# Hybrid encoder layer: another form of the bidirectional scan's inner products, and its state products in each other's banks

## Chip, cores and metric

One Trainium2 chip, one core. The metric is device time in microseconds (us) for one execution of the program.

## What is computed

One encoder layer on x of 1024 tokens × 1024 features, fp32. After an RMSNorm one projection gives all mixers their columns. Mixer A is a convolution branch. Mixer B, which this change is about, is a gated linear recurrence in both directions, with 8 heads of 128 features. Then both are gated, merged and projected, and a feed-forward layer with a short convolution and a last RMSNorm follow. The recurrence, per head and direction:

```python
f = lb + (1.0 - lb) * sigmoid(z);  f = clip(f, 1e-6, 1.0)      # one forget value per token and feature
k = (1.0 - lb) * sigmoid(-z);      q = silu(q) * 128 ** -0.5
S_t = diag(f_t) S_{t-1} + k_t v_t^T                            # 128 x 128 state
o_t = S_t^T q_t                                                # forward + backward (tokens flipped)
o = o * rsqrt(mean(o * o) + 1e-6) * norm_w * silu(og)          # per head, then @ o_w
```

So token t sees token s through q_t · (the product of all f between them) · k_s, per feature.

## The kernel before, in words

**Dense work.** Projections are matmuls of 128x128 weights by 128x512 tokens. Each fp32 operand is split into a high and a low part and multiplied in three terms (`mm3`, L148 to L150). The matmul of 128x512 is about 0.39 us in the trace. Much of the dense work (merge gates and the convolution branch's projection) is kept as a stream, `dense`, which hands out *pieces*; a piece is two steps of k, six matmuls. `dense.fill(n)` runs n pieces, with fractions carried over.

**The scan.** 8 heads × 2 halves of 512 tokens make 16 *units*. Features lie in partitions, tokens along the free axis, both directions side by side (128 x 2 x 512). A unit has these parts:

- `scan_inputs` loads q and z (SP's queue), makes f (sigmoid, then Identity with scale and bias on ScalarE, ACT; clip on VectorE, DVE, L1103) and k (sigmoid of −z, L1093 to L1096).
- `scan_base` (DVE) works in blocks of 8 tokens: running products of f inside a block (`DE`), their reciprocal (L1127), q and k scaled by them (`Qh`, and `Kh` at L1074), then q and k decayed to the block's edges (`qF`, `kG`) and the blocks' totals `tb`. It is a generator of 12 steps. All products go through the helper at L1071.
- `scan_levels` puts together the 32x32 and larger blocks of the token × token matrix. `inside` (L1203) multiplies `Qh` and `Kh` per 32 tokens for both directions. Then come levels h = 8, 16, 32, 64: at each, the second half of a block of 2h tokens sees the first half, and the reverse. Levels 8 and 16 need k in an order of its own, which ACT copies into a page `A` (L1189, two pages) and 16 small matmuls read (L1191); levels 32 and 64 multiply directly (`blocks`, L1217), after a matmul by zeros (`none`, L1241) has cleared the bank. After each level, `kG`, `qF` and `tb` are doubled to the next block size (L1071). Masks choose which product goes where in `D_t` (L1255 to L1261), and ACT puts `D_t` on the diagonal of the matrix `S_t` (L1263, four copies at L1265).
- `scan_states` transposes `kG` (L1275, ACT copies the result at L1277) and multiplies by v (L1284). The forward product goes into bank `ob`, from which DVE makes the states `Sf` (L1290, L1292). The backward product goes into `sc`, from which ACT copies `Sb` (L1302, L1304).
- `scan_outputs`, once per head, multiplies S_t by v and q by the states (L1325), ACT copies and squares the result (L1327, L1330), GpSimd (POOL) makes the root of the mean (`rstd_small`, L519 and L520), ACT scales (L1344), PE transposes (L1351), DVE gates (L1353).

**Order.** TensorE's (PE) instructions run in the order in which the program writes them. The other engines' orders are chosen by a scheduler that estimates times; it keeps the data's order. Every generator's `yield` is a *filler place*: the loop calls `between(FILL)` there, which lets in dense pieces, steps of the next unit's base (`BASE_STEPS`) and one step of the last head's outputs:

```python
def between(fill):
    dense.fill(fill)
    if ahead is not None:
        ahead.step(BASE_STEPS)
    pending.fill(1)
```

`scan_levels` has four places and `scan_states` three, with FILL = 1.265 pieces each; ahead of the first unit stands `dense.fill(21)`. Outputs of a head run in the places of the next head's first unit and into its second.

**PSUM.** 8 banks of 128x512: three for dense products (`mm`), two `sc`, two `tr` (transposes), one `ob`. A bank is written again only when its readers are done; with one bank of a kind, the next writer waits for the last reader.

Of the kernel before, what the change touches and what calls it, by code (L numbers as in the profile page):

```python
# [10 lines left out]
F32 = mybir.dt.float32  # L11
F32R = mybir.dt.float32r
I32 = mybir.dt.int32
U8 = mybir.dt.uint8
# [5 lines left out]
FILL = 1.265  # L20
# [10 lines left out]
BASE_STEPS = 2  # L31
# [16 lines left out]
def tile_hybrid_encoder(  # L48
# [877 lines left out]
    m_f, m_b, m_d, m_16 = [cp.tile([P, 32], U8, name=n) for n in ("m_f", "m_b", "m_d", "m_16")]  # L926

    def build_masks():
# [7 lines left out]
        fs = mp.tile([P, 4, 32], F32, tag="tm", name=nm("fs"), bufs=4)  # L936
        V.tensor_copy(fs[:, 0, :], xo)
        V.tensor_tensor(fs[:, 1, :], it, ip, op=ALU.subtract)
        ge = fs[:, 1, :]
        V.tensor_scalar(m_d, fs[:, 0, :], 0.0, None, op0=ALU.is_equal)  # L940
        V.tensor_scalar(m_16, fs[:, 0, :], 16.0, None, op0=ALU.is_ge)
        V.tensor_scalar(fs[:, 2, :], fs[:, 0, :], 8.0, None, op0=ALU.is_lt)
        V.tensor_scalar(fs[:, 3, :], ge, 0.0, None, op0=ALU.is_ge)
        V.tensor_tensor(m_f, fs[:, 2, :], fs[:, 3, :], op=ALU.mult)
        V.tensor_scalar(fs[:, 3, :], ge, 0.0, None, op0=ALU.is_lt)
        V.tensor_tensor(m_b, fs[:, 2, :], fs[:, 3, :], op=ALU.mult)
# [111 lines left out]
    NB = H // 8  # L1058
    DE = hp.tile([P, 2, 2, H], F32, name="DE")
    dg = hp.tile([P, 4, 32], F32, name="dg")  # L1060
    none = hp.tile([P, 32], mybir.dt.bfloat16, name="none")
    E0, D0 = 0, 2 * H
    for o in (E0 + 3, D0 + 3):
        G.memset(view(DE, o, [[8, 2 * NB]]), 1.0)
    G.memset(none, 0.0)
    G.memset(dg, 0.0)

    N2 = 2 * NB

    def tt(o, a, b, op=ALU.mult):  # L1070
        V.tensor_tensor(o, a, b, op=op)  # L1071

    def keys(o, a, scale, b):
        V.scalar_tensor_tensor(o, a, scale, b, op0=ALU.mult, op1=ALU.mult)  # L1074
# [7 lines left out]
    def scan_inputs(i):  # L1082


        h, half = divmod(i, 2)
        q = page(hp, "q", 2)
        f = hp.tile([P, 2, H], F32, tag="f", name=nm("f"), bufs=2)
        kk = hp.tile([P, 2, H], F32, tag="k", name=nm("k"), bufs=2)
        nc.sync.dma_start(q, d_q[h][half])
        for d in range(2):  # L1090
            z = page(hp, "zi", 3)
            nc.sync.dma_start(z, d_z[d][h][half])
            A.activation(kk[:, d, :], z, AF.Sigmoid, scale=-1.0)  # L1093
            A.activation(z, z, AF.Sigmoid)
            fo = view(f, d * H + 7 * d, [[8, NB], [1 - 2 * d, 8]])
            A.activation(  # L1096
                fo,
                z.rearrange("p (b e) -> p b e", e=8),
                AF.Identity,
                scale=oml_of(d, h),  # L1100
                bias=lb_of(d, h),
            )
        V.tensor_scalar(f, f, MIN_FORGET, 1.0, op0=ALU.max, op1=ALU.min)  # L1103
        return q, f, kk, kscale[:, h : h + NH + 1 : NH]

    def scan_base(ins):


        q, f, kk, ks = ins

        def two(t, *r):
            if len(r) == 1:
                return view(t, r[0], [[8, N2]])
            return view(t, r[0], [[r[1] - r[0], 2], [8, N2]])

        fv = lambda *r: two(f, *r)
        ed = lambda *r: two(DE, *r)
        D = D0


        V.tensor_copy(ed(2, D + 4), fv(3, 4))
        tt(ed(1, D + 5), fv(2, 4), fv(3, 5))
        yield
        tt(ed(0, D + 6), fv(1, 6), ed(1, D + 5))
        tt(ed(D + 7), ed(D + 6), fv(7))
        yield
        V.reciprocal(ed(D, 7), ed(0, D + 7))  # L1127
        yield

        fm = hp.tile([P, 2, NB], F32, tag="fm", name=nm("fm"), bufs=2)  # L1130
        turned = view(fm, NB, [[-NB, 2], [1, NB]])
        tt(turned, view(f, 0, [[H, 2], [8, NB]]), view(DE, E0, [[H, 2], [8, NB]]))
        tb = hp.tile([P, 3, NB], F32, tag="tb", name=nm("tb"), bufs=3)
        tt(tb[:, 0:2, :], turned, view(DE, D + 7, [[H, 2], [8, NB]]))
        V.tensor_copy(tb[:, 2, :], tb[:, 0, :])
        tt(ed(D + 1, 6), ed(D, 7), fv(1, 7))
        yield
        tt(ed(D + 2, 5), ed(D + 1, 6), fv(2, 6))
        tt(ed(4), ed(5), fv(5))
        yield  # L1140

        qF = hp.tile([P, 2, H], F32, tag="qF", name=nm("qF"), bufs=3)
        kG = hp.tile([P, 2, H], F32, tag="kG", name=nm("kG"), bufs=2)
        Qh = hp.tile([P, 2, H], F32, tag="Qh", name=nm("Qh"), bufs=1)
        Kh = hp.tile([P, 2, H], F32, tag="Kh", name=nm("Kh"), bufs=1)
        along = [[8, NB], [1, 8]]
        for d in range(2):
            m0, st = ((0, 1), (7, -1))[d]
            whole = [[8, NB], [st, 8]]
            tt(view(Qh, (1 - d) * H + m0, whole), view(q, m0, whole), view(DE, D + d * H, along))  # L1150
            yield
            keys(
                view(Kh, d * H + m0, whole),
                view(kk, d * H + m0, whole),
                ks[:, d : d + 1],
                view(DE, d * H, along),
            )
            yield
        both = [[H, 2], [8, NB], [1, 8]]
        tt(view(qF, 0, both), view(Qh, 0, both), view(fm, 0, [[NB, 2], [1, NB], [0, 8]]))  # L1160
        yield
# [662 lines left out]
```

## Time and profile before

| | |
|---|---|
| Three runs, device time | 1775.28 us median (1771.59 to 1776.22) |
| The profiled execution | 1770.28 us, span 1768.5 us, granted clock 0.998 |
| PE, DVE, ACT, POOL in the 16 units (512.78 to 879.60 us) | 346.56, 325.83, 210.87, 13.81 us of 366.82 us |
| DVE busy, whole span | 1251.3 us (71%) |

A row of the profile's groups gives line, engine, operation, output and input tiles, shape and count; behind the bar busy us, the mean of one in ns, and idle time of the engine just before them with what ended it. In a timeline row the first number is the start, the second the duration, and brackets hold the wait before it. PE records an fp32 matmul as two instructions. PE, DVE and the granted clock in tenths, in forty equal slices of the span:

```profile
PE   8999999999999899999999999999999999999997
DVE  5599999646789989998555566766676667444455
PEclk9999999999999999999999999999999999999999
```

The units of the scan lie in slices 12 to 20 of these 40 (44 us each). DVE shows 8 and 9 in slices 12 to 19 and 5 in slice 20, in which the last unit runs without a next one's base.

### The profile page before, as it was taken

The page shows a single profiled execution, that of the slowest core. Times are in us where ns is not written, and L with a number is a line of the kernel's source. Part 1 is how long each engine was busy: PE and PEld are TensorE (multiplying, and loading weights), DVE is VectorE, ACT ScalarE, POOL GpSimd, SP SyncE. Part 2 cuts the span into 40 slices and gives each one's busy share as a digit, 9 for nine tenths or more (in the row PEclk, how much of TensorE's full clock was granted, in tenths as well). Part 3 has the DMA queues.
Part 4 walks back from the last instruction along what each step waited for, and adds up shares of the span by engine and source line. Part 5 has one row for each costly group of instructions (what it writes and reads, how often), then busy time and mean ns, then how long its engine had stood idle before and what let it go on. Part 6 is the DMA issues. An engine that isn't in the chain of part 4 may idle for free.

```text
span 1768.5 us, 28121 instructions
## 1 busy us (share of the span) xinstructions
PE 1721.4 (97%) x10854; PEld 1410.2 (80%) x10854; DVE 1251.3 (71%) x1886; ACT 774.1 (44%) x1486; POOL 160.3 (9%) x174
## 2 busy tenths in 40 slices
PE   8999999999999899999999999999999999999997
PEld 6878888787877787877878887788888888888885
DVE  5599999646789989998555566766676667444455
ACT  7444443334565655655551344443444344422223
POOL 2201111100000000000000002111111111000000
PEclk9999999999999999999999999999999999999999
DMA  8778878846653333435377665576776675433233
GB/s 285 241 169 185 199 179 208 197 143 203 208 175 107 127 106 112 126 109 180 132 233 215 200 206 170 152 162 145 153 158 148 148 147 139 155 104 124 75 92 137
DMA packets 321836, 285.37 MB, mean 161 GB/s; under 512 B 15006, under 2 KB 242086, under 8 KB 321702
## 3 DMA queue, kind: packets, MB, share of 16 engines
q1 hardware_dynamic: 277878, 248.96, 44.5%
q0 software_dynamic: 43824, 34.61, 13.5%
q8 instruction: 85, 1.39, 0.3%
q14 instruction: 49, 0.40, 0.1%
HBM read 189.40 MB, written 76.81 MB: 151 GB/s over the span
## 4 chain that ended last, share of the span: by engine, by line
PE 70%; DVE 14%; DMA 6%; ACT 5%; issue 3%; POOL 1%; SPq 0%; POOLq 0%; ACTq 0%; DVEq 0%
PE mm L148 16%; PE mm L150 16%; PE mm L149 16%; PE sc L148 4%; PE sc L150 4%; PE sc L149 4%; DVE DE L1071 2%; PE tr L148 2%; PE tr L150 2%; PE tr L149 2%; DVE qF L1071 2%; DVE kG L1071 2%; DVE wp L124 2%; DMA wr<-in_w_in_dram 1%; DVE Kh L1074 1%
## 5 line engine op out<-in xcount | busy, mean ns | idle before, releaser
L148 PE MATMUL mm<-hx,wp 128*128 128x512 f32 x1144 | 460.3, 402 | 5.6 <-ACT tm L778 1.8
L150 PE MATMUL mm<-hx,wp 128*128 128x512 f32 x1144 | 447.4, 391 | 1.2 <-DVE wp L124 1.1
L149 PE MATMUL mm<-hx,wp 128*128 128x512 f32 x1144 | 446.2, 390 | 0.0
L124 ACT CAST wp<-wr 128x1024 fp32r<-128x1024 f32 (+2 forms) x171 | 162.0, 948 | 357.0 <-PE mm L149 249.1
L148 PEld LDWEIGHTS mm<-hx,wp 128*128 128x128 f32 x1144 | 214.9, 188 | 51.7 <-DVE ev L727 2.7
L150 PEld LDWEIGHTS mm<-hx,wp 128*128 128x128 f32 x1144 | 214.7, 188 | 50.3 <-DVE wp L124 4.2
L149 PEld LDWEIGHTS mm<-hx,wp 128*128 128x128 f32 x1144 | 215.1, 188 | 41.4 <-issue 0.7
L124 DVE TENSOR_TENSOR wp<-wr,wp 128x1024 fp32r<-128x1024 f32 (+2 forms) x169 | 186.7, 1105 | 76.0 <-ACT wp L124 75.6
L966 DVE SCALAR_TENSOR_TENSOR acc<-gl,v_b,acc 128x1024 f32<-128x1024 f32 x120 | 148.9, 1279 | 0.4
L1675 DVE TENSOR_TENSOR xr<-mm,xr 128x512 f32<-128x512 f32 x48 | 33.2, 691 | 72.7 <-PE mm L150 72.7
L376 ACT COPY su<-mm 128x512 f32<-128x512 f32 x82 | 47.5, 579 | 59.7 <-PE mm L150 59.7
L124 ACT CAST wq<-sw 128x1024 fp32r<-128x1024 f32 x41 | 43.1, 1051 | 57.4 <-PE mm L149 35.7
L1524 DVE SCALAR_TENSOR_TENSOR tm<-gp,v_a,tm 128x512 f32<-128x512 f32 x88 | 66.0, 750 | 1.8
L148 PE MATMUL mm<-hy,wp 128*128 128x512 f32 x164 | 64.5, 393 | 0.0
L148 PE MATMUL tr<-hx,wp 128*128 128x512 f32 x164 | 64.3, 392 | 0.0
L149 PE MATMUL mm<-hy,wp 128*128 128x512 f32 x164 | 64.2, 392 | 0.0
L148 PE MATMUL sc<-hy,wq 128*128 128x512 f32 x164 | 64.2, 392 | 0.0
L150 PE MATMUL sc<-hy,wq 128*128 128x512 f32 x164 | 64.2, 391 | 0.0
L150 PE MATMUL tr<-hx,wp 128*128 128x512 f32 x164 | 63.8, 389 | 0.0
L149 PE MATMUL tr<-hx,wp 128*128 128x512 f32 x164 | 63.8, 389 | 0.0
L149 PE MATMUL sc<-hy,wq 128*128 128x512 f32 x164 | 63.8, 389 | 0.0
L150 PE MATMUL mm<-hy,wp 128*128 128x512 f32 x164 | 63.7, 388 | 0.0
(362 smaller groups left out, 3411.1 us busy)
## 6 DMA issues: line engine op xcount, KB each, us to landing
wr<-in_w_in_dram SPq DMA_DIRECT2D x48, 512.0 KB, 4.7
wr<-in_ffn_w_up_dram SPq DMA_DIRECT2D x24, 512.0 KB, 4.8
sw<-in_ffn_w_up_dram SPq DMA_DIRECT2D x44, 256.0 KB, 2.8
d_g<-ft SPq DMA_DIRECT2D x44, 256.0 KB, 3.1
sw<-in_ffn_w_up_dram POOLq DMA_DIRECT2D x20, 512.0 KB, 8.3
sw<-in_w_in_dram SPq DMA_DIRECT2D x38, 256.0 KB
wr<-sw POOLq DMA_DIRECT2D x33, 256.0 KB, 3.2
wr<-wr POOLq DMA_DIRECT2D x33, 256.0 KB, 3.6
```

Of the source, the lines that this page charges most:

```text
L124: parts = A.copy(hi, src), eng.tensor_tensor(lo, src, hi.bitcast(F32), op=ALU.subtract)
L148: T.matmul(acc, whi[:, k, :], ahi, start=first, stop=False, skip_group_check=again)
L149: T.matmul(acc, whi[:, k, :], alo, start=False, stop=False, skip_group_check=again)
L150: T.matmul(acc, wlo[:, k, :], ahi, start=False, stop=last, skip_group_check=again)
L376: A.copy(t, acc)
L966: V.scalar_tensor_tensor(acc, g[:, k : k + S], tap(k), acc, op0=ALU.mult, op1=ALU.add)
L1071: V.tensor_tensor(o, a, b, op=op)
L1074: V.scalar_tensor_tensor(o, a, scale, b, op0=ALU.mult, op1=ALU.mult)
L1524: V.scalar_tensor_tensor(c, g[:, o + k : o + k + H], vec("fdw", k * NF + j), c, op0=ALU.mult, op1=ALU.add,)
L1675: V.tensor_tensor(xr[i][half], acc, xr[i][half], op=ALU.add)
```

## The change

- The scan's inside is built another way: instead of blocks of 8 with running products and a reciprocal, the halving of the levels goes down to h = 1. Levels 1, 2, 4, 8, 16, 32, 64 are all alike: `kG` and `qF` are doubled in place seven times each, and totals halve in number. The tokens' own products (`k_d`) use the sum of both directions' keys.
- Operands of levels 1 to 8, and keys of 16, are *woven* by ACT into contiguous pages (L1094 of the new kernel; eight pages `A` in rotation). For level 1 the queries come from a product of DVE.
- `scan_base` now has five steps: inputs of level 1 and its doubling; 2; four groups of 16 small matmuls (own, 1, 2, 4) into the four slots of one `sc` bank; the copy to `D_t` with three masked copies; the weaving of 16. So the next unit's first levels run inside the current unit. `scan_levels` begins with levels 8 and 16 in one `ob` bank (L1113), then 32, then 64: three places; `scan_states` has two (both transposes together). FILL is 1.77 and BASE_STEPS 1; at the start 7 pieces, then five steps with 3, 4, 4, 3, 0 pieces.
- The four diagonal copies of ACT become four DMAs on ACT's queue (L1226).
- The forward state product goes into `sc`, the backward one into `ob` (`Sf` at L1251 and L1253, `Sb` copies at L1263 and L1265 of the new kernel); the second transpose uses an `mm` bank in place of `tr` (L1236, copied at L1238); v is transposed one place earlier.
- Masks m_1, m_2, m_8 in place of m_f, m_b; three `D` tiles, three `kG`, four `qF`; f is written contiguously by ACT.

In the new kernel the product helper is L1062, the clip L1084, `blocks` L1196, the level matmuls L1113, the scalings of keys L1142, masked copies L1177 and L1214, outputs L1286, their scaling L1305.

```diff
-FILL = 1.265
+FILL = 1.77
-BASE_STEPS = 2
+BASE_STEPS = 1
...
-        kk = hp.tile([P, 2, H], F32, tag="k", name=nm("k"), bufs=2)
+        kG = hp.tile([P, 2, H], F32, tag="kG", name=nm("kG"), bufs=3)
         nc.sync.dma_start(q, d_q[h][half])
         for d in range(2):
             z = page(hp, "zi", 3)
             nc.sync.dma_start(z, d_z[d][h][half])
-            A.activation(kk[:, d, :], z, AF.Sigmoid, scale=-1.0)
+            A.activation(kG[:, d, :], z, AF.Sigmoid, scale=-1.0)
             A.activation(z, z, AF.Sigmoid)
-            fo = view(f, d * H + 7 * d, [[8, NB], [1 - 2 * d, 8]])
-            A.activation(
-                fo,
-                z.rearrange("p (b e) -> p b e", e=8),
-                AF.Identity,
-                scale=oml_of(d, h),
-                bias=lb_of(d, h),
-            )
+            A.activation(f[:, d, :], z, AF.Identity, scale=oml_of(d, h), bias=lb_of(d, h))
         V.tensor_scalar(f, f, MIN_FORGET, 1.0, op0=ALU.max, op1=ALU.min)
-        return q, f, kk, kscale[:, h : h + NH + 1 : NH]
+        return q, f, kG, kscale[:, h : h + NH + 1 : NH]
+
+    def pairs(t, h, other=H):
+
+        return view(t, 0, [[other + h, 2], [2 * h, H // (2 * h)], [1, h]])
+
+    def woven(t, h):
+
+        t_h = page(hp, "A", 8)
+        A.copy(pairs(t_h, h, 0), pairs(t, h))
+        return t_h
+
...
+    def level(b, A_t, Q_t):
+        for at, g, o in each():
+            T.matmul(b[g, o], A_t[:, at : at + 32], Q_t(at), start=True, stop=True)
+
+    def row(t):
+        return lambda at: t[:, at : at + 32]
+
+    def double_keys(kG, tb, h):
+        n, nb = H // (2 * h), H // h
+        tt(pairs(kG, h), pairs(kG, h), view(tb, 1, [[nb - 1, 2], [2, n], [0, h]]))
+
+    def double_queries(qF, q, tb, h):
+        n, nb = H // (2 * h), H // h
+        tt(pairs(qF, h), q, view(tb, nb + 1, [[-(nb + 1), 2], [2, n], [0, h]]))
+
+    def totals(tb, h, to=None):
+        n, nb = H // (2 * h), H // h
+        tn = None
+        if to is None:
+            tn = hp.tile([P, 2, n], F32, tag=f"tb{h}", name=nm("tb"), bufs=1 if h < 8 else 2)
+            to = view(tn, 0, [[n, 2], [1, n]])
+        tt(to, view(tb, 0, [[nb, 2], [2, n]]), view(tb, 1, [[nb, 2], [2, n]]))
+        return tn
     def scan_base(ins):
...
+        q, f, kG, ks = ins
+        qF = hp.tile([P, 2, H], F32, tag="qF", name=nm("qF"), bufs=4)
+        D_t = hp.tile([P, 4, 32], F32, tag="D", name=nm("D"), bufs=3)
+        for d in range(2):
+            V.tensor_scalar(kG[:, d, :], kG[:, d, :], ks[:, d : d + 1], None, op0=ALU.mult)
+        k_d, Q1 = page(hp, "A", 8), page(hp, "A", 8)
+        tt(k_d, kG[:, 0, :], kG[:, 1, :], ALU.add)
+        A1 = woven(kG, 1)
+        odd = H // 2
+        tt(
+            pairs(Q1, 1, 0),
+            view(q, 0, [[1, 2], [2, odd], [1, 1]]),
+            view(f, H, [[1 - H, 2], [2, odd], [1, 1]]),
+        )
+        tt(
+            view(qF, 1, [[H - 1, 2], [2, odd]]),
+            view(q, 1, [[-1, 2], [2, odd]]),
+            view(f, H + 1, [[-(H + 1), 2], [2, odd]]),
+        )
+        double_keys(kG, f, 1)
+        double_queries(qF, pairs(Q1, 1, 0), f, 1)
+        tb = totals(f, 1)
         yield
...
+        A2, Q2 = woven(kG, 2), woven(qF, 2)
+        double_keys(kG, tb, 2)
+        double_queries(qF, pairs(qF, 2), tb, 2)
+        tb = totals(tb, 2)
+        A4, Q4 = woven(kG, 4), woven(qF, 4)
         yield
...
+        b = bank("sc")
+        for n, (k_t, q_t) in enumerate(((k_d, q), (A1, Q1), (A2, Q2), (A4, Q4))):
+            level(slot(b, n), k_t, row(q_t))
+        double_keys(kG, tb, 4)
+        double_queries(qF, pairs(qF, 4), tb, 4)
+        tb = totals(tb, 4)
+        A8, Q8 = woven(kG, 8), woven(qF, 8)
         yield
...
+        A.copy(D_t, near(slot(b, 3)))
+        for n, m in enumerate((m_d, m_1, m_2)):
+            V.copy_predicated(D_t, over(m), near(slot(b, n)))
+        double_keys(kG, tb, 8)
+        double_queries(qF, pairs(qF, 8), tb, 8)
+        tb = totals(tb, 8)
+        A16 = woven(kG, 16)
         yield
...
+        yield qF, kG, tb, D_t, A8, Q8, A16
     def scan_levels(base, S_t, Tt):
...
+        def double(tb, h, to=None):
+            double_keys(kG, tb, h)
+            double_queries(qF, pairs(qF, h), tb, h)
+            return totals(tb, h, to)
+
+        b = bank("ob")
+        level(slot(b, 0), A8, row(Q8))
+        level(slot(b, 1), A16, lambda at: view(qF, at, [[H + 16, 2], [1, 16]]))
+        tb = double(tb, 16)
+        for n, m in enumerate((m_8, m_16)):
+            V.copy_predicated(D_t, over(m), near(slot(b, n)))
+        yield
         b = bank("sc")
...
+        for at, g, _ in each():
+            T.matmul(b[g, at : at + 32], none, none, start=True, stop=True)
+        blocks(b, 32)
+        tb = double(tb, 32)
+        yield
+        blocks(b, 64)
+        double(tb, 64, view(Tt, 0, [[4, 2], [1, 4]]))
+        A.copy(S_t, c4(b))
+        for g in range(0, P, 32):
+            nc.scalar.dma_start(S_t[g : g + 32, :, g : g + 32], D_t[g : g + 32])
+        yield
     def scan_states(i, kG, v, Tt, Sf, Sb):
         half = i % 2
         kTs = []
         for d in range(2):
-            b = bank("tr")
+            b = bank("mm" if d else "tr")
             for c in range(4):
                 T.transpose(b[:, c * P : (c + 1) * P], kG[:, d, c * P : (c + 1) * P], ident)
             kT = page(hp, "kT", 2)
             A.copy(kT, b)
             kTs.append(kT)
-            yield
+        yield
         for d in range(2):
-            u = bank("sc" if d else "ob")
+            u = bank("ob" if d else "sc")
             for c in range(4):
                 sl = slice(c * P, (c + 1) * P)
                 T.matmul(u[:, sl], kTs[d][:, sl], v[:, c, :], start=True, stop=True)
...
     NI = 2 * NH
     cur = Base(scan_inputs(0))
     ins = scan_inputs(1)
-    dense.fill(21)
+    dense.fill(7)
+    for pieces in (3, 4, 4, 3, 0):
+        cur.step(1)
+        dense.fill(pieces)
     pending = Stream(iter(()))
     for h in range(NH):
         Tt = hp.tile([P, 2, 2, 4], F32, tag="Tt", name=nm("Tt"), bufs=3)
...
             S_t = hp.tile([P, 4, P], F32, tag="S", name=nm("S"), bufs=3)
             vl = load(d_v[h][half])
             for n, _ in enumerate(scan_levels(base, S_t, Tt[:, half])):
-                if n == 2:
+                if n == 1:
                     b = bank("tr")
                     for c in range(4):
                         T.transpose(b[:, c * P : (c + 1) * P], vl[:, c * P : (c + 1) * P], ident)
                     v = hp.tile([P, 4, DK], F32, tag="v", name=nm("v"), bufs=3)
                     A.copy(v.rearrange("p c e -> p (c e)"), b)
                 between(FILL)
-            qF, kG = base[0], base[1]
+            qF, kG = base[:2]
             for _ in scan_states(i, kG, v, Tt, Sf, Sb):
                 between(FILL)
             kept.append((S_t, v, qF))
```

157 lines of the change are left out of this document (20 added, 137 removed).

## Prediction, made before the changed kernel ran

> **What bounds the kernel now.** I read the page first, then a window of the scan, then the instructions inside it.
>
> ```profile
> span 1768.5 us, 28121 instructions
> PE 1721.4 (97%) x10854; PEld 1410.2 (80%) x10854; DVE 1251.3 (71%) x1886; ACT 774.1 (44%) x1486; POOL 160.3 (9%) x174
> PE 70%; DVE 14%; DMA 6%; ACT 5%; issue 3%; POOL 1%; SPq 0%; POOLq 0%; ACTq 0%; DVEq 0%
> ```
>
> TensorE is busy for 97% of the span: a change can win only the 47 us of its idle time, or its own work. DVE holds 14% of the chain that ended last although it is busy for 71% only; so there is a stage in which it is late. The first matmul of each unit's levels (L1203) marks where a unit begins. The windows between those marks have, from left: length, busy us and instructions of PE, weight load, DVE, ACT, POOL, then clock, DMA share and GB/s.
>
> ```profile
> 512.78:879.60 366.82, 346.56 (x4760) 284.94 (x4760) 325.83 (x673) 210.87 (x522) 13.81 (x14) 1.00 0.37 122
> 577.67:598.50 20.83, 19.33 (x280) 15.60 (x279) 20.76 (x41) 11.62 (x24) 0.00 (x0) 1.00 0.49 153
> 598.50:627.20 28.70, 24.64 (x324) 20.66 (x323) 23.79 (x50) 18.29 (x50) 2.64 (x2) 1.00 0.28 90
> 719.39:739.35 19.96, 19.52 (x279) 15.48 (x278) 19.93 (x40) 11.03 (x23) 0.00 (x0) 1.00 0.54 171
> 831.39:855.88 24.49, 24.37 (x323) 20.73 (x322) 18.27 (x45) 15.24 (x46) 1.83 (x2) 1.00 0.24 84
> ```
>
> The first row is all 16 units: PE idles 366.82 − 346.56 = 20.26 us there, 43% of all its idle time in 21% of the span. In a second unit of a head (577.67, 719.39) DVE is busy 20.76 of 20.83 and 19.93 of 19.96 us: it is the bound. First units carry the last head's outputs too; DVE has some room there, and PE lost 4.06 us in one and 0.12 us in the other. The timeline of PE shows what ends the idle time:
>
> ```profile
> 602.22 0.46 PE L1191 MATMUL ob<-qF,A 128*32 128x32 f32 x32 [1.10 <-DVE qF L1071]
> 602.61 0.50 PE L148 MATMUL mm<-hx,wp 128*128 128x512 f32 x1
> 605.28 0.46 PE L1325 MATMUL ob<-v,S 128*128 128x128 f32 x2 [1.02 <-DVE D L1260]
> 618.42 0.66 PE L1275 MATMUL tr<-ident,kG 128*128 128x128 f32 x4 [1.94 <-DVE kG L1071]
> ```
>
> It is DVE's decayed q and k (and what is queued behind them) that PE waits for. So the change is priced in two currencies: PE time, which counts fully, and DVE time, which counts through those 20 us.
>
> **DVE, removed and added.** Columns of a group: busy us, mean ns, idle before it.
>
> ```profile
> L1071 DVE TENSOR_TENSOR qF<-qF,tb 128x512 f32<-128x512 f32 x64 | 43.9, 686 | 0.2 <-PE sc L1191 0.2
> L1071 DVE TENSOR_TENSOR kG<-kG,tb 128x512 f32<-128x512 f32 x64 | 43.8, 685 | 8.2 <-ACT A L1189 7.3 <-PE sc L1217 0.8
> L1127 DVE RECIPROCAL DE<-DE 128x256 f32<-128x256 f32 x15 | 26.3, 1753 | 0.2
> L1074 DVE SCALAR_TENSOR_TENSOR Kh<-k,kscale,DE 128x512 f32<-128x512 f32 x31 | 23.1, 745 | 0.0
> L1071 DVE TENSOR_TENSOR DE<-DE,f 128x256 f32<-128x256 f32 x30 | 19.8, 661 | 0.1
> L1260 DVE COPY_PREDICATED D<-m,ob 128x128 f32<-128x128 uint8 x16 | 4.8, 300 | 0.0
> L1261 DVE TENSOR_TENSOR D<-D,dg 128x128 f32<-128x128 f32 x16 | 4.6, 288 | 0.0
> L1071 DVE TENSOR_TENSOR tb<-tb 128x96 f32<-128x96 f32 x15 | 3.8, 252 | 0.0
> L1071 DVE TENSOR_TENSOR Tt<-tb 128x8 f32<-128x8 f32 x16 | 2.6, 161 | 0.0
> L1103 DVE TENSOR_SCALAR f<-f 128x1024 f32<-128x1024 f32 x14 | 9.7, 690 | 1.4 <-ACT f L1096 1.4
> ```
>
> All instructions of L1071 in that window, as one row of the windows view for that line (busy DVE us and count):
>
> ```profile
> 512.78:879.60 366.82, 205.74 (x367) 1.00 0.37 122
> ```
>
> Before, per unit: L1071, reciprocals and keys are (205.74 + 26.3 + 23.1) / 15.5 = 16.5 us (the window holds 16 sets of level operations and some 15 of base operations), four predicated copies 1.20, the add 0.29: 18.0 us. Left alone are the clip (L1103) and the state updates.
>
> After, per unit: 18 products of 512 elements: the two of q with f, the sum of both keys, seven doublings of kG, seven of qF, the first totals. 18 × 0.686 = 12.35. Six smaller totals of 256 to 8 elements: from the rows with 8 (161 ns), 96 (252) and 512 (686) the slope is near 1.04 ns an element, so 0.42 + 0.29 + 0.22 + 0.19 + 0.18 + 0.16 = 1.46. Two scalings of kG by kscale, 128x512, not in the trace in that form: between 0.35 (half of the clip's 690) and 0.745 (keys with a second tensor), I take 0.5: 1.0. Five predicated copies 1.50. Sum 16.3 us. This adds durations, which overlap when operations follow each other directly:
>
> ```profile
> 589.23 0.68 DVE L1071 TENSOR_TENSOR kG<-kG,tb 128x512 f32<-128x512 f32 x1
> 589.83 0.68 DVE L1071 TENSOR_TENSOR qF<-qF,tb 128x512 f32<-128x512 f32 x1
> ```
>
> Starts 0.60 apart for 0.68: 0.08 less for each of 31 operations is 13.8 us. The saving lies between 18.0 − 16.3 = 1.7 and 18.0 − 13.8 = 4.2; the first row counted overlaps half, and I take **3 us a unit**. DVE in second units goes from 20.0–20.8 us to about 17–17.8 against some 19.7 of PE: it stops being the bound, and up to 20 us of PE's idle time is free to go.
>
> One price is uncertain. The first level works with a stride of 8 bytes. The only strided rows, 128x256 with a stride of 32 bytes, took 661 ns where the slope gives 420, but the 96-element row, read with a stride of 8 bytes, lies on the slope. I take no surcharge; the other end, the same surcharge (240 ns per 256 elements, so 0.48) on the five operations of the first level, is 2.4 us a unit. The Trainium skill ("SBUF — State Buffer", specifications and the cacheline note) has lines of 16 bytes that want two hits each, which an 8-byte stride gives; by it the surcharge is nil, and 96 elements in 252 ns agree.
>
> **PE.** Start times give what small matmuls take:
>
> ```profile
> 598.50 0.73 PE L1203 MATMUL sc<-Qh,Kh 128*32 128x32 f32 x62
> 599.08 0.45 PE L1191 MATMUL sc<-qF,A 128*32 128x32 f32 x30
> 599.46 0.50 PE L148 MATMUL mm<-hx,wp 128*128 128x512 f32 x1
> L149 PE MATMUL mm<-hx,wp 128*128 128x512 f32 x1144 | 446.2, 390 | 0.0
> ```
>
> Each fp32 matmul leaves two records. 48 matmuls (inside and level 8) take 599.46 − 598.50 = 0.96 us, 20 ns each; level 16 took 0.39 (602.22 to 602.61), 24 ns each. Before: 1.35 us a unit. After: 64 in one bank (four levels) at 19 to 20 ns, 1.24, and 32 in ob, 0.67: 1.91. So +0.56 us a unit, **+9 us**. The Trainium skill ("TensorE: Matmul & The Clock Gate", "Wait — 56ns, not 53.3ns?") says that starts never come closer than about 25 ns; 32 more matmuls by that would be 12.8 us in place of 9. The row with 20 ns goes below it, so I stay with the rows. Dense pieces: 7 places × 1.265 = 8.86 before, 5 × 1.77 = 8.85 after, and 7 + 14 in place of 21 at the start, so the same dense work. But the first matmul of a visit shows 0.50 where the mean is 0.39; two visits fewer per unit give 2 × 0.11 × 16 = **−3.5 us**. Level 32, level 64, transposes, products and outputs keep their counts. PE net: +5.5 us.
>
> **ACT and the banks.**
>
> ```profile
> L1189 ACT COPY A<-kG 128x512 f32<-128x512 f32 x32 | 19.7, 616 | 13.9 <-DVE kG L1071 13.9
> L1265 ACT COPY S<-D 32x128 f32<-32x128 f32 x64 | 18.8, 293 | 1.0
> L1302 ACT COPY Sb<-sc 128x384 f32<-128x384 f32 x16 | 7.6, 475 | 3.8 <-PE sc L1284 3.6
> 849.23 0.20 POOL L519 TENSOR_SCALAR ors<-oss 128x8 f32<-128x8 f32 x1 [42.15 <-ACT jk L1330]
> 849.50 1.63 POOL L520 TENSOR_TENSOR ors<-ors,mhalf 128x8 f32<-128x8 f32 x1
> 851.17 1.28 ACT L1344 ACTIVATE tm<-tm,ors 128x128 f32<-128x128 f32 x4 [0.31 <-POOL ors L520]
> 609.25 0.32 SPq L1089 DMA_DIRECT2D q<-d_q  x1
> ```
>
> Page copies: eight per unit in place of two, +6 × 0.616 = 3.7 us; four diagonal copies of 0.293 go, −1.17. In their place ACT's queue issues four DMAs; a DMA issue took 0.32 us on SP's queue, none is shown on ACT's: +1.3. ACT in a first unit goes from 15.2–18.3 to 19–22 of 24.5, in a second from 11 to 15 of 20. It doesn't become the bound by busy time, but it runs in order, and three things now hang on it.
>
> (1) kG and qF are doubled in place, so each doubling waits until ACT has woven the old values: eight copies a unit, before two. Two a unit gave DVE 7.3 us of waiting in all (the kG row). Four times that is 29 us at most, on a DVE that has 3 us × 16 = 48 us of new room; I take 5 us that reach PE. (2) The product for the backward states now lies in ob, the only bank of its kind, and the next unit's levels 8 and 16 need it empty: they wait for ACT's copies to Sb (0.475 each). In seven first units those stand behind the scalings that wait for POOL: 849.23 to 851.17, then 1.28, then 0.475, 3.7 us, with one or two dense pieces (1.4 us each) for cover. That leaves 0.9 to 2.3 us if both chains begin together, less if POOL's begins earlier, as it mostly does: 0.7 × 7 = 5 us, bounds 0 and 16. Before, the copy read sc, which has two banks. (3) The diagonal DMAs, behind ACT's queue, feed outputs that come about a unit (20 us) later; nothing waits for them as long as ACT isn't more than that behind. Queued behind their issue are the next woven copies: in (1).
>
> kT of the backward direction takes a bank of the dense product (mm) and waits at worst for one 0.58 us eviction, 0 to 9 us; three banks rotate there, so 1 us. Masks are built before the scan, beside dense work: nothing.
>
> **Sum.** From 1770.28 us (span 1768.5 and 1.8 around it): PE +5.5; idle in the scan −20.3, given back 5 + 5 + 1 = 11. Net −3.8, so 1766.5 in a profiled execution. The three runs' median, 1775.28, lies 5.0 above this execution; on it the forecast is **1771 us**. Idle between 6 and 17 us gives 1766 to 1777.
>
> **Rivals.**
> - **The waits for ACT vanish** in the dense pieces: idle falls to 4 us, 5.5 − 16 = −11, 1764. For it: DVE's 3 us of room per unit, second units with ACT at 15 of 20. Against: eight in-place copies.
> - **ACT's order becomes the bound (slower).** Place: first units. Sigmoids for the unit after next, woven copies, four DMA issues and squares stand in one queue, and the POOL-gated scalings stop all of it; the woven copies behind are late, DVE's doublings with them, then PE's levels and transposes. If one stop of 1.94 us (849.23 to 851.17) reaches PE in each of 16 units it is 31 us idle against 20.3: 5.5 + 11 = +16, 1791; if every first unit loses 3.7 and second units 0, 26 us, +11, 1786. It decides when idle exceeds 15 us. For it: the 28.70 us unit, where PE lost 4 us with ACT at 18.29. Against: the 24.49 one, where it lost 0.12 with the same chain.
> - **Strided operations cost double:** 2.4 of the 3 us saved are gone, DVE remains at the bound, the 20 us stay: +5.5 and part of (1) and (2), about 1783.
>
> **How the numbers follow.** Forecast 0.47, waits vanish 0.18, ACT's order 0.28, strides 0.07. What a measurement can tell from no change is 0.3%, 5.3 us: below 1770 faster, above 1780.6 slower. The forecast's own range, 1766 to 1777, gives 0.19 faster and 0.26 same and 0.02 slower; the first rival 0.18 faster; the others 0.35 slower. In all 0.37, 0.26, 0.37. The range, 1760 to 1789, leaves out the ends of the first two rivals.
>
> **What would show it.** Right: in windows of second units PE is at 97% or more and DVE near 85%; the waits view has the ob level's matmul (L1113) waiting for ACT's Sb copy (L1263), in first units, about 5 us in all, and DVE's L1062 waiting for the woven copies (L1094); PE busy in the scan is 352 us. Wrong: PE busy above 358 (small matmuls dearer); DVE still at 95% in second units (strides, or the scaling at 0.75); PE's L1113, L1196 or L1236 waiting above 17 us in all (ACT's order); or waits of L1286 for the diagonal DMAs, which I priced at nothing.

## The result, and the profile after

| | before | after |
|---|---|---|
| device time, median of 10 runs each | 1772.23 us (1770.65 to 1776.76) | 1768.34 us (1767.30 to 1771.54) |
| the profiled execution, and its span | 1770.28, 1768.5 us | 1768.21, 1766.4 us |

The ratio is 0.9975, with a 95% interval of 0.9965 to 0.9984: the change is worth a quarter of a per cent, 4 us. The seven further runs of the kernel before, which came with the result, moved its median from 1775.28 to 1772.23; so the absolute forecast of 1771, which was the earlier median less 3.8, was 2.7 us too high, while the difference was 3.9 us against a forecast of 3.8. The two profiled executions differ by 2.1 us only.

The page of the changed kernel: span, busy time of the engines, chain that ended last by engine.

```profile
span 1766.4 us, 30281 instructions
...
PE 1728.3 (98%) x11878; PEld 1422.8 (81%) x11878; DVE 1206.5 (68%) x1839; ACT 808.0 (46%) x1518; POOL 158.4 (9%) x171
...
PE 82%; ACT 5%; DVE 4%; DMA 4%; issue 3%; POOL 1%; ACTq 0%; SPq 0%; POOLq 0%; DVEq 0%
```

DVE's part of the chain fell from 14% to 4%, ACT's stayed at 5%. PE is busier by 7 us, as new matmuls were added, and the span is nonetheless shorter: idle time went. To compare stages, two PE instructions that both kernels have serve as marks, a statistics matmul at 465.57 us (L528) and one at 1081.50 us (L538); between them lies all that was changed. The windows view of before, then of after (PE, weight load, DVE, ACT, POOL, clock, DMA share, GB/s):

```profile
465.57:1081.50 615.93, 593.75 (x5860) 487.94 (x5859) 473.95 (x885) 316.40 (x701) 19.82 (x23) 1.00 0.51 162
```

```profile
465.99:1077.20 611.21, 599.93 (x6883) 499.82 (x6882) 428.60 (x837) 351.05 (x733) 18.13 (x20) 1.00 0.53 165
```

The stage is 4.72 us shorter. PE's busy time rose by 6.2 us and its idle time fell from 22.18 to 11.28, by 10.9. DVE lost 45.4 us, ACT gained 34.7. The time ahead of the stage differs by 0.4 us. The part behind it took 687.0 us before and 689.2 after; in the twelve experiments, none of which edits anything there, it took 685.6 to 691.3, so 2 us there is spread. I call this *the stage* below and give its PE idle time for each kernel. Two units of the changed kernel, a first (646.53) and a second one (716.67), between starts of the matmuls of L1113 in `ob`:

```profile
646.53:672.03 25.50, 23.05 (x377) 19.82 (x376) 18.21 (x44) 15.77 (x43) 1.83 (x2) 1.00 0.35 108
...
716.67:738.07 21.40, 20.47 (x348) 16.57 (x347) 18.44 (x39) 17.05 (x36) 0.00 (x0) 1.00 0.45 136
```

In the second unit DVE is busy 18.44 of 21.40 us, 86%; over the seven second units with a next one's base it is 82 to 96%, where all but the last were at 99% or more before. PE is busy for all of two of these seven and for 92 to 96% of the other five. What PE waits for in the scan now (total us, times, longest):

```profile
PE ob L1113 <- ACT Sb L1263: 3.8, 3, 2.5
PE sc L1196 <- DVE qF L1062: 3.6, 7, 1.0
PE sc L1245 <- ACT kT L1238: 2.0, 2, 1.3
PE ob L1113 <- ACT Sb L1265: 0.5, 2, 0.3
```

The old waits for DVE's kG and qF are a quarter of what they were (before, 14.2 us at L1275, L1217 and L1191), and the level in `ob` waits for ACT's copies to Sb: the new wait that the bank swap brought. The longest one, 2.46 us, can be followed on ACT's timeline and then PE's:

```profile
666.45 1.05 ACT L124 CAST wp<-wr 128x1024 fp32r<-128x1024 f32 x1
668.60 1.28 ACT L1305 ACTIVATE tm<-tm,ors 128x128 f32<-128x128 f32 x4 [1.10 <-POOL ors L520]
669.78 0.61 ACT L1082 ACTIVATE zi<-zi 128x512 f32<-128x512 f32 x1
670.30 0.61 ACT L1081 ACTIVATE kG<-zi 128x512 f32<-128x512 f32 x1
670.82 0.80 ACT L1083 ACTIVATE f<-zi,lbw 128x512 f32<-128x512 f32 x1
671.52 0.46 ACT L1263 COPY Sb<-ob 128x384 f32<-128x384 f32 x1
```

```profile
667.13 1.06 PE L1245 MATMUL ob<-v,kT 128*128 128x128 f32 x8
667.95 0.48 PE L148 MATMUL mm<-hx,wp 128*128 128x512 f32 x1
...
672.03 0.46 PE L1113 MATMUL ob<-A,A 128*32 128x32 f32 x32 [2.46 <-ACT Sb L1263]
```

The product was ready by 668.2. ACT stood for 1.10 us until POOL had its root, ran four scalings, then three operations on a later unit's inputs, and only then the copy that empties `ob`; PE's one dense piece of cover was long over. The next one, 1.06 us at 533.93, lies in the first head, when no outputs are pending and nothing waits for POOL; the other three are 0.28 us each.

The two waits for kT stand right behind the diagonal DMAs, as in this one, on ACT's queue and then PE's:

```profile
588.82 3.24 ACTq L1226 DMA_DIRECT2D S<-D  x3
594.40 0.58 ACT L1238 COPY kT<-tr 128x512 f32<-128x512 f32 x1
595.04 1.16 PE L1245 MATMUL sc<-v,kT 128*128 128x128 f32 x8 [1.29 <-ACT kT L1238]
```

ACT issued DMAs for 3.2 us, then made the copies that had become due, and came to kT late.

### The profile page after: what moved, and what is told of

Its sections match the earlier page's. It is cut to its first block, busy times and chain, and to the rows that moved or that the text cites. A ratio compares the mean times of both kernels' runs of the same rounds, so it can differ in the third digit from the quotient of the medians.

```text
span 1766.4 us, 30281 instructions
## 1 busy us (share of the span) xinstructions
PE 1728.3 (98%) x11878; PEld 1422.8 (81%) x11878; DVE 1206.5 (68%) x1839; ACT 808.0 (46%) x1518; POOL 158.4 (9%) x171
## 4 chain that ended last, share of the span: by engine, by line
PE 82%; ACT 5%; DVE 4%; DMA 4%; issue 3%; POOL 1%; ACTq 0%; SPq 0%; POOLq 0%; DVEq 0%
PE mm L148 19%; PE mm L150 19%; PE mm L149 19%; PE sc L148 4%; PE sc L150 4%; PE sc L149 4%; PE ob L1286 2%; PE tr L148 2%; PE tr L150 2%; PE tr L149 2%; PE sc L1113 1%; DMA tm<-d_bm 1%; POOL ors L520 1%; PE sc L1196 1%; DMA sw<-in_ffn_w_up_dram 1%
## 5 line engine op out<-in xcount | busy, mean ns | idle before, releaser
L148 PE MATMUL mm<-hx,wp 128*128 128x512 f32 x1144 | 457.5, 400 | 6.1 <-ACT su L376 2.9
L148 PEld LDWEIGHTS mm<-hx,wp 128*128 128x128 f32 x1144 | 215.0, 188 | 53.0 <-ACT su L376 3.3
L1062 DVE TENSOR_TENSOR qF<-qF,tb 128x512 f32<-128x512 f32 x96 | 65.4, 689 | 15.5 <-ACT A L1094 14.0
L1062 DVE TENSOR_TENSOR kG<-kG,tb 128x512 f32<-128x512 f32 x96 | 65.9, 689 | 5.1 <-PE sc L1196 4.8
L148 PE MATMUL mm<-hy,wp 128*128 128x512 f32 x164 | 64.5, 393 | 0.0
L148 PE MATMUL tr<-hx,wp 128*128 128x512 f32 x164 | 64.3, 392 | 0.0
L148 PE MATMUL sc<-hy,wq 128*128 128x512 f32 x164 | 64.2, 392 | 0.0
L149 PE MATMUL mm<-hy,wp 128*128 128x512 f32 x164 | 64.2, 392 | 0.0
L150 PE MATMUL sc<-hy,wq 128*128 128x512 f32 x164 | 64.2, 391 | 0.0
```

The lines of the kernel that those rows point to most:

```text
L148: T.matmul(acc, whi[:, k, :], ahi, start=first, stop=False, skip_group_check=again)
L149: T.matmul(acc, whi[:, k, :], alo, start=False, stop=False, skip_group_check=again)
L150: T.matmul(acc, wlo[:, k, :], ahi, start=False, stop=last, skip_group_check=again)
```

## The experiments

**Theory.** DVE was the bound of second units; taking 45 us off it frees some 16 us of PE's idle time, of which new waits at ACT give 5 back, and added small matmuls cost PE 9 us less 3.5. **Rivals.** The gain is one of order (fewer filler places, inner levels a unit earlier), not of DVE's load; the swap of banks is a gain and not a cost; small matmuls only fill time in which PE would have waited. Each ratio below is to the kernel before, on the same chip, with its 95% interval; the changed kernel's is 0.9975.

**1. Banks as before.**

```diff
-            u = bank("ob" if d else "sc")
+            u = bank("sc" if d else "ob")
```

> The changed kernel with the state products' banks as before (forward in ob, backward in sc). Theory: the level in ob no longer waits for ACT's Sb copies (4.3 us in the changed trace); it now waits for DVE's chain of four state updates, about 1.3 us after the product, with 1.4 to 2.8 us of dense pieces for cover and a DVE that has room, so under 1 us in all. 1768.3 - 3 = 1765, between 1763 and 1768. Rival, that the swap is a part of the gain because DVE frees ob late: the wait on Sb goes, one on the Sf updates of 5 to 10 us comes, 1770 to 1775.

Measured 0.9956 (0.9943 to 0.9969), 0.0019 or 3.4 us under the changed kernel; the intervals overlap a little, but the trace points the same way: PE's stage idle went from 11.28 to 9.19 us, and its waits are

```profile
PE sc L1196 <- DVE qF L1062: 3.4, 6, 1.0
PE ob L1113 <- DVE Sf L1253: 2.5, 6, 0.9
PE ob L1245 <- ACT kT L1238: 1.1, 1, 1.1
```

The wait for Sb is gone and one for Sf takes its place, larger than the 1 us that I gave it and smaller than what went. The swap costs, here and again between 2 and 5 below (0.9956 and 0.9924); it isn't part of the gain.

**2. The diagonal by ACT's copies, no DMA.**

```diff
-            nc.scalar.dma_start(S_t[g : g + 32, :, g : g + 32], D_t[g : g + 32])
+            A.copy(S_t[g : g + 32, :, g : g + 32], D_t[g : g + 32])
```

> The changed kernel with ACT's four copies on the diagonal of S_t in place of the four DMAs. Theory (ACT is not the bound and the DMAs wait for nothing that matters): four copies of 0.29 us against four issues of about the same, 1768 plus or minus 2. Rival, ACT's order is what is left over: its 5.7 us of idle ahead of woven copies that end with the DMA S<-D vanish, PE's waits for L1196 and L1113 fall by half, 1764 to 1766; or, the other way, the 1.2 us of busy time per unit on ACT show as waits, 1771 to 1774.

Measured 0.9956 (0.9944 to 0.9968), again 3.4 us under the changed kernel, so the theory's "no difference" was wrong here. The reason stands in the trace of the changed kernel, in the line of the DMAs (minimum, median, maximum ns on ACT's queue; then who waited for them, us and times):

```profile
L1226 ACTq DMA_DIRECT2D S<-D x64: 592/608/1910, 522.3 to 864.3; - x64
...
  ACT A L1094: 5.7, 2
```

One issue holds ACT's queue for 0.61 us, twice a copy of 0.29. Such time isn't counted as busy, so ACT's 351 us of the stage hide another 64 × 0.61 = 39 us. With the copies ACT shows 369 us and is yet freer: PE's waits for kT are gone, and DVE waits 4.0 us for woven copies, 14.0 in the changed kernel. Stage idle 7.72 us.

**3. As much DVE work again.**

```diff
+        tt(load_t, load_t, load_t)
```

stands five times in each `scan_base`; `load_t` is a 128x512 tile of ones.

> The changed kernel with five more products of 128x512 per unit on DVE, on a tile that nothing else reads: 3.0 us a unit by start times, as much as I said the change saves there. Theory (the idle time of PE in the scan came from DVE at its bound): DVE is back at 95% or more of second units, PE's idle time in the stage between the two statistics matmuls goes from 11.3 us back by 6 to 10, 1774 to 1778. Rival (the gain is from fewer filler places and from inner levels made a unit earlier, not from room on DVE): idle 11 to 13 us, 1768 to 1771.

Measured 1.0025 (1.0011 to 1.0039), 0.0050 or 8.9 us over the changed kernel. The products were written five to a unit, but the scheduler, for which nothing else depends on them, put all 80 between 485.6 and 717.9 us, into the first nine units. That makes the run its own control. Below, the stage is cut where the tenth unit begins (L1113 in `ob`), for the changed kernel and then for this one:

```profile
465.99:716.67 250.68, 244.05 (x3566) 203.38 (x3564) 197.15 (x423) 170.21 (x363) 7.47 (x9) 1.00 0.47 145
716.67:1077.20 360.53, 355.88 (x3319) 296.44 (x3319) 231.46 (x414) 180.85 (x371) 10.66 (x11) 1.00 0.58 179
```

```profile
468.03:728.79 260.76, 248.49 (x3565) 206.93 (x3563) 243.47 (x503) 171.44 (x363) 10.16 (x10) 0.98 0.45 139
728.79:1089.30 360.51, 355.93 (x3320) 296.61 (x3320) 231.40 (x414) 180.64 (x371) 10.66 (x11) 1.00 0.58 179
```

Where DVE was loaded, PE's idle time rose from 6.63 to 12.27 us; behind it, it is 4.58 and was 4.65. So the load does it, with 5.6 us in all (stage idle 16.85), just under the theory's 6 to 10. The other 4.4 us are PE's busy time: the granted clock is 0.98 in this part. From 584.2 to 587.6 and from 679.8 to 686.6 us it was 0.50, each time behind a stop of PE (1.83 and 4.88 us). Where PE waits was not foreseen (line numbers behind L1163 are shifted by up to 8):

```profile
PE ob L1113 <- ACT Sb L1271: 10.2, 5, 4.9
PE sc L1204 <- DVE qF L1062: 3.4, 4, 1.4
```

It isn't DVE that PE names but ACT. ACT's waits in the same run say why: its woven copies wait longer for DVE's kG (33.8 us, 21.4 in the changed kernel), and the copies to Sb stand behind them.

**4. Two groups of small matmuls less.**

```diff
-        for n, (k_t, q_t) in enumerate(((k_d, q), (A1, Q1), (A2, Q2), (A4, Q4))):
+        for n, (k_t, q_t) in ((0, (k_d, q)), (3, (A4, Q4))):
...
-            V.copy_predicated(D_t, over(m), near(slot(b, n)))
+            V.copy_predicated(D_t, over(m), near(slot(b, 0)))
```

> The changed kernel without the matmuls of levels 1 and 2 (the masked copies read the group of the tokens' own products for them): 32 small matmuls less per unit. By the rows, 0.62 us a unit: 9.9 us, 1758. At 25 ns each 12.8 us, 1755.5. Rival: these matmuls only fill time in which PE would wait for DVE or ACT anyway, so that 3 us or less come out, 1765 to 1768.

Measured 0.9923 (0.9910 to 0.9936), 0.0052 or 9.2 us under the changed kernel: they cost PE fully, near the 9.9 by the rows. Stage idle stayed at 11.27 us, so they filled nothing.

**5. Both: banks as before, and ACT's copies.** The diffs of 1 and 2.

> The changed kernel with both the old banks of the state products and the old diagonal copies. If the two costs are separate (PE's wait for Sb was 3.3 us still when the DMAs were gone, and the DMA issues were still there when the banks were back), the gains add: 0.9975 less 0.0019 twice, ratio to before 0.9937, about 1761. Rival, that both are one cost (ACT's queue is late, and Sb with it): 0.995 to 0.9956, as each alone.

I call this kernel *version 5*. Measured 0.9924 (0.9910 to 0.9938), 1758.09 us: faster than the kernel before by 0.76% and than the changed kernel by about 0.5%, 9 us. The gains add, or more. Stage idle is 4.16 us, and in the waits view of the scan this is all that is left:

```profile
PE sc L1196 <- DVE qF L1062: 3.2, 6, 1.0
PE ob L1113 <- DVE Sf L1253: 0.3, 1, 0.3
```

PE's busy time in the stage fell too, to 597.50 from 599.93. Two rows of PE's timeline show where, the inner levels' last 96 records and what follows, in the changed kernel and here:

```profile
706.12 1.18 PE L1113 MATMUL sc<-A,A 128*32 128x32 f32 x96
707.26 0.46 PE L1286 MATMUL ob<-v,S 128*128 128x128 f32 x2
```

```profile
701.31 1.07 PE L1113 MATMUL sc<-A,A 128*32 128x32 f32 x96
702.32 0.49 PE L1286 MATMUL ob<-v,S 128*128 128x128 f32 x2
```

1.14 us against 1.01. With the copies it is 1.00 in all 16 units, here and in 2; with the DMAs the median is 1.14, whichever queue issues them (10). Over 16 units that is 2 us. It comes with the DMAs; how they hold up the group stays open.

**6 and 9. The kernel before, with less on DVE.** In both the base leaves work out after the first unit; 9 leaves out more.

```diff
-        V.reciprocal(ed(D, 7), ed(0, D + 7))
+        if first:
+            V.reciprocal(ed(D, 7), ed(0, D + 7))
```

and in 9 also

```diff
-        tt(ed(D + 1, 6), ed(D, 7), fv(1, 7))
+        if first:
+            tt(ed(D + 1, 6), ed(D, 7), fv(1, 7))
...
-        tt(ed(D + 2, 5), ed(D + 1, 6), fv(2, 6))
+        if first:
+            tt(ed(D + 2, 5), ed(D + 1, 6), fv(2, 6))
```

> The kernel before without the reciprocal (it runs in the first unit only, so later units scale q and k with products that were not inverted): 1.75 us a unit less on DVE, on no other engine. Theory (DVE at its bound makes PE's 22 us of idle time in the stage): 15 times 1.6 is 24 us less on DVE, about half of which PE gets back, 8 to 13 us, ratio 0.993 to 0.9955. Rival (PE waits for the order and latency of a chain through ACT, not for DVE's load): within 3 us, 0.998 to 1.

> The kernel before, where after the first unit the base leaves out the reciprocal and two strided products of 256 (its outputs are then scaled wrongly): 1.75 + 2 x 0.66 = 3.1 us a unit less on DVE, 46 us in all, as much as the change takes off DVE in the stage (45 us). If DVE's load is what made PE idle, this gives what the change gave without its new waits: PE idle in the stage from 22.2 to between 6 and 12 us, ratio 0.9915 to 0.9945. If the change's own order (inner levels a unit earlier, a base of five steps) did it, this stays near the run without the reciprocal alone (18.0 us idle, 0.9966): idle 14 to 18, 0.995 to 0.997.

Measured 0.9966 (0.9953 to 0.9979) and 0.9939 (0.9923 to 0.9956). DVE in the stage fell by 22.4 and by 36.9 us (the second less than the 46 expected), PE's idle time from 22.18 to 18.02 and to 12.32:

```profile
466.29:1076.80 610.51, 592.49 (x5860) 488.06 (x5859) 451.51 (x869) 316.04 (x700) 18.85 (x23) 1.00 0.51 163
```

```profile
466.17:1071.10 604.93, 592.61 (x5860) 488.45 (x5859) 437.08 (x840) 316.03 (x701) 18.85 (x23) 1.00 0.52 164
```

The first, 6 us by its ratio, lies between the 8 to 13 us of the theory and the 3 us of the rival, and alone decides nothing. The second ends at 12.32, just above the 6 to 12 expected, with a ratio inside the theory's range. So DVE's load alone, with the old order untouched, gives back 9.9 us of idle time, nearly the 10.9 of the change; the return isn't even: 0.19 us per us of DVE for the first 22, 0.39 for the next 14.

**7. The kernel before, with only the banks swapped.**

```diff
-            u = bank("sc" if d else "ob")
+            u = bank("ob" if d else "sc")
```

> The kernel before with only the banks of the two state products swapped. Theory (the swap costs where a level in ob opens the next unit): here the ob level stands one filler place later, behind 1.7 us more of dense work, so nothing or up to 2 us slower, ratio 0.999 to 1.0015. Rival (the swap is a gain of its own, since the backward copy has a bank to itself): 2 to 5 us faster, 0.997 to 0.999.

Measured 0.9998 (0.9986 to 1.0009): nothing. Where a filler place stands between the product and the next `ob` level, the swap costs nothing, and it gains nothing.

**8. More DVE work and the old banks together.** The diffs of 3 and 1.

> The changed kernel with five more products per unit on DVE, and the banks of the state products as before. With the load alone PE's longest wait was for ACT's Sb copies in ob (10.2 us of some 15), behind woven copies that were late because DVE was. If that is the way by which DVE's load costs, most of it goes with the banks back: 0.996 to 0.998 (1765 to 1769). If a full DVE costs PE by itself, the waits move to DVE's Sf and doubled q: 1.000 to 1.0025 (1772 to 1777).

Measured 1.0015 (1.0001 to 1.0030), 0.0010 under 3, within both intervals; the load lies in the first nine units here too, and the stage idle is 16.01 us. The wait changed its name only:

```profile
PE ob L1113 <- DVE Sf L1261: 8.6, 8, 3.3
PE sc L1204 <- DVE qF L1062: 4.3, 6, 1.3
```

The second reading holds: a full DVE costs PE by itself, since whoever empties the single `ob` bank, ACT behind DVE or DVE itself, is late.

**10. The diagonal DMAs from SP's queue.**

```diff
-            nc.scalar.dma_start(S_t[g : g + 32, :, g : g + 32], D_t[g : g + 32])
+            nc.sync.dma_start(S_t[g : g + 32, :, g : g + 32], D_t[g : g + 32])
```

> The changed kernel with the four diagonal DMAs issued from SP's queue in place of ACT's. If the cost of the DMAs is the issue on ACT (0.6 us each there), the gain is that of the copies: 0.9956, about 3 us under the changed kernel. If it is the transfer or its semaphores (the group of inner levels took 0.12 us longer per unit with the DMAs), most of it stays: 0.997 to 0.998. Slower than the changed kernel (0.998 to 1.000) if SP's loads, which stand in order behind them, come late.

Measured 0.9949 (0.9935 to 0.9963): as with the copies. The issue is as long on SP, where nobody waits for it:

```profile
L1226 SPq DMA_DIRECT2D S<-D x64: 585/594/2027, 523.2 to 863.1; - x64
```

The stage, with the DMAs on SP and then with the copies (2):

```profile
466.86:1076.70 609.84, 601.72 (x6883) 501.35 (x6882) 427.06 (x837) 351.39 (x733) 18.13 (x20) 1.00 0.53 165
466.96:1072.50 605.54, 597.82 (x6883) 498.65 (x6882) 427.29 (x837) 369.44 (x797) 18.39 (x20) 1.00 0.53 165
```

PE's idle time fell from 11.28 to 8.12 us, near the 7.72 of the copies. As with these, both waits for kT are gone and DVE's wait for woven copies is small, 2.8 us. This part of the cost is the issue on ACT. PE's busy time didn't fall: the group of small matmuls keeps its 1.14 us, a cost of the DMAs on either queue, and 3.4 us at a granted clock of 0.50 (671.9 to 675.3, behind the stop for Sb) come on top. The ratio agrees with that of the copies all the same, and a good part of this run's gain lies behind the stage (685.9 us against 689.2), where the spread is. So the time alone doesn't tell the two apart.

**11. No root on POOL.**

```diff
-        rstd_small(rs, ss, DK)
+        A.copy(rs, ss)
```

> The changed kernel with ACT's copy of the sums of squares in place of POOL's root of their mean (outputs are scaled wrongly): the scalings no longer wait for POOL (9.3 us of ACT's idle time). By my step, Sb's copies are late because they stand behind those scalings: PE's wait for Sb in ob falls from 4.3 us to 1.5 or less and the time by 2 to 4 us, ratio 0.995 to 0.9965. Rival (they stand behind woven copies that wait for DVE): the wait stays at 3 to 4.5 us, 0.997 to 0.9985.

Measured 0.9905 (0.9891 to 0.9918), 12 us under the changed kernel where 2 to 4 were expected. PE's wait for Sb fell from 4.3 to 2.2 us, so half of it, not most, stood behind POOL (the longest went from 2.46 to 0.79 us; the one in the first head stayed, 1.15), and the waits for DVE's qF, 3.6 us, went as well:

```profile
PE ob L1113 <- ACT Sb L1263: 1.9, 2, 1.1
PE ob L1113 <- ACT Sb L1265: 0.3, 1, 0.3
```

The stage was 7.9 us shorter, with 4.25 us idle: whatever stands behind the gated scalings was late, and DVE behind it. It isn't the woven pages (DVE waits 14.3 us for them, as before) but the next inputs' sigmoids: DVE's wait for kG from L1081 fell from 18.0 to 10.8 us. The other 4 us lie mostly behind the stage (685.6 us against 689.2), inside the spread that part shows in all kernels; I don't explain them.

**12. Version 5 with a later scaling.** One more `yield` between POOL's root and the scalings.

```diff
         rstd_small(rs, ss, DK)
         yield
         yield
+        yield
```

> The changed kernel with the old banks of the state products, the diagonal copies on ACT, and one more filler place between POOL's root and the scalings. The two first alone left 4.2 us of PE's idle time in the stage and 10.8 us in which ACT stood before a scaling until POOL was done. If that standing still costs PE (without the root the changed kernel gained 12 us), ACT's wait for POOL falls to 4 to 8 us and the time by 1 to 4 us, ratio 0.990 to 0.992. Rival, that with banks and copies back nothing of PE hangs on that wait any more: 0.992 to 0.9935.

Measured 0.9986 (0.9972 to 1.0001): a miss, and slower than version 5. ACT's wait for POOL fell, to 6.8 us, as expected. But the last head's outputs come a step later too, behind the scan, where the list of dense pieces for cover was left as it was:

```profile
PE mm L148 <- ACT hx L124: 10.6, 1, 10.6
```

PE stood 10.6 us, from 894.5 to 905.1, for the operand made from these outputs. The granted clock was halved from 897.2 to 910.8 us, so that PE's first 5.7 us behind the stop went at half; version 5 has 1.00 there.

```profile
897.20:910.80 13.60, 5.70 (x13) 4.13 (x14) 7.92 (x12) 4.78 (x9) 0.00 (x0) 0.50 0.86 263
```

In the scan itself the later scaling brought nothing: from 468 to 850 us PE idled 3.70 us, and 3.79 in version 5. That is the rival's case, that with banks and copies back nothing of PE hangs on that wait.

## Why the prediction was right, step by step

**DVE's saving**, 3 us a unit: 45.4 us in the stage, 2.8 a unit. No surcharge for the stride of 8 bytes, as I took it; the scalings of keys, taken at 0.5, were 0.484. The first row has no stride, the second reads at 8 bytes:

```profile
L1062 DVE TENSOR_TENSOR A<-kG 128x512 f32<-128x512 f32 x16 | 11.0, 689 | 9.1 <-PE sc L1113 9.0
...
L1062 DVE TENSOR_TENSOR A<-q,f 128x512 f32<-128x512 f32 x16 | 11.0, 688 | 0.0
```

By the rule of the Trainium skill that the prediction gave ("SBUF — State Buffer", specifications and the cacheline note) such a stride costs nothing, and these rows agree.

**PE's work**, +5.5 us: busy time +6.2. Of its two terms, 9 us for small matmuls is nearer 9 to 12: by start times the last 48 of a unit's 64 took 1.14 us in the changed kernel and 1.01 in version 5, the first 16 another 0.28 in both; 1.42 and 1.29 against my 1.24. Experiment 4 puts 32 of them at 9.2 us. The 25 ns floor that the Trainium skill gives ("TensorE: Matmul & The Clock Gate", "Wait — 56ns, not 53.3ns?") is not seen: 48 in 1.01 us are 21 ns each. The visits' term, −3.5, is −2.8: L148, the first matmul of each k step, took 423 ns in the mean of 358 before and 415 of 362 after, where its steady value is 391; 11.5 us against 8.7.

**Idle time**, −20.3 + 11 = −9.3 us: −10.9. That DVE's load makes PE idle is shown from both sides: 9 takes it off the kernel before, and 3 puts it on the changed one, where idle time came back in the loaded units and in no others. It isn't shown that it is all of the 10.9. In the first nine units of 3 the changed kernel idles 12.27 us at 243.47 us of DVE, and the kernel before, up to the same mark (719.39), 14.23 at 225.01; a share of the new order isn't excluded.

**The 11 given back** came out in its sum, and with its parts that is luck.

- The `ob` wait was to be 5 us, 0.7 in each of seven first units behind POOL. It was 4.3, but 2.46 of that in one such unit, 1.06 in the first head, where POOL has no part, and 0.28 three times.
- The doublings behind woven copies were to cost PE 5 us. DVE waited 14.0 us for these copies, but not ahead of PE's waits for qF: with the DMAs off ACT's queue DVE's wait fell to 4.0 and 2.8 us (2 and 10), and PE's stayed at 3.4 and 3.2, from 3.6. Ahead of them DVE runs back to back in the timeline, or has waited for ACT's sigmoids and casts. What reached PE of the late woven copies is at most the 2.0 us at kT, behind the DMA issues.
- For the `mm` bank it was 1 us; no wait of L1236 shows.

**What failed is one term**: the DMAs, whose issue on ACT was taken at SP's 0.32 us for a plain load, and so at no difference to the copies. They took 0.61, and with what they delay cost 3.4 us by the ratio of 2. In the stage of its trace, the shortest of its five executions, 5.7 us are gone: 3.6 us of PE's idle time, most of which the queue decides (3.2 in 10), and 2.1 of PE's busy time in the group of small matmuls, which the prediction doesn't have. The sum came out because the idle term was a little better than I had it.

**The signs.** DVE came to the 85% named for second units, with a wide spread; PE's 97% was reached in two of seven. PE is busy for 355.03 us from 514.71 to 879.60, about the stretch of the 16 units, between the 352 forecast and the 358 that would have said wrong.

**The rivals.** "Waits for ACT vanish" is version 5: idle 4.16 us, which I had put at 4, but only after two parts of the change were undone. "ACT's order becomes the bound" didn't happen in the changed kernel. In 3, with DVE loaded again, PE named ACT (10.2 us); but when DVE empties the bank in ACT's place, nearly all the idle time stays (8). So there ACT passes on what DVE is late with, and the rival isn't shown.

## What to carry to other kernels

Where the last reader of a single buffer stands in an engine's queue behind other work and behind waits for a third engine, these set the buffer's time: before swapping buffers, look at who empties each and at what stands ahead of it, and give the buffer that opens the next round to the reader with nothing ahead of it. Small DMAs aren't free of their issuing engine; count their issue as busy time of it, and move them to a queue with nothing to do, or copy. A load put into a kernel as a test stands where the scheduler puts it: look in the trace before reading the result. A change that moves the time by little can hold a gain and two losses: undo its parts one by one.

## What the runs showed of the hardware

A DMA issue of 32 partitions × 4 × 32 elements, from SBUF to SBUF, took 0.61 us on ACT's queue and 0.59 on SP's, while a load of 128x512 took 0.32 on SP's. So the length goes with the transfer and not with the queue; which of its properties counts isn't shown.

PE's granted clock was halved for short stretches behind some of its stops: 3.4 us in 3 behind a stop of 1.83 us, 3.4 us in 10 behind 2.45, 6.8 us in 3 behind 4.88, 13.6 us in 12 from within the stop of 10.6 us on. The stop of 2.46 us in the changed kernel was followed by no such stretch, so the length of a stop alone doesn't decide it. A mean over a long window hides them: over the whole stage, 3 shows 0.99.

```profile
679.80:686.60 6.80, 5.65 (x75) 4.63 (x76) 5.58 (x11) 4.34 (x10) 0.00 (x0) 0.50 0.28 80
```
